# The end of a two-layer decoder trunk: the last add and square in halves, other sums and the norm weight ahead, stores on two queues

## The chip, the cores and the metric

The kernel runs on one core of a Trainium2 chip. The time is device microseconds of one execution; several executions are timed and their median is taken. A change of about 0.2% (4.55 us) is what a measurement of this kernel can tell from no change.

## The reference

Input x is 256 tokens by 2048 columns in float32, with float32 weights. Layer 0 is a norm, gated linear attention, a residual add, a norm, a SwiGLU network (width 5632) and a residual add. The stream is then normed once more and projected to keys and values that layer 1 shares. Layer 1 is a norm, stick-breaking attention, a residual add, and again a norm, a SwiGLU network and a residual add. A last norm gives the output. What matters here is the very end:

```
def rmsnorm(x, w):
    xf = xf * lax.rsqrt(jnp.mean(xf * xf, axis=-1, keepdims=True) + EPS)
    return xf.astype(x.dtype) * w
...
        h = h + swiglu(rmsnorm(h, ffn_norm_w[layer]), ffn_w_gate_up[layer], ffn_w_down[layer])
...
    return rmsnorm(h, final_norm_w)
```

The last norm needs the sum of squares of all 2048 columns of a token before any output column can be scaled, and the last columns come out of the last matmuls.

## The kernel before, in words

The 256 tokens are two token tiles of 128 (index t), one token per partition; the residual stream h stays on the chip as 128 x 2 x 2048, and its 2048 columns are worked on in four column blocks of 512 (index nb, or b).

Every weight comes from memory once, in loads of 512 KB (`load_w`, line 115, issued by SyncE into `raw`). Each float32 weight is split into a rounded part and a rest: ScalarE (ACT) casts `raw` to `hi` (line 119), VectorE (DVE) subtracts to get `lo` (line 120). A product is then three matmuls on TensorE: hi by hi, hi by lo, lo by hi, added up in a PSUM tile `acc`. `raw` has four buffers, `hi` and `lo` three each, so ACT and DVE run up to two loads ahead of TensorE and then wait until TensorE has freed a buffer.

In the SwiGLU network the hidden width is taken in three passes; the third ends with the down projection of its part. That down projection runs over the four column blocks (`residual_gemm`). For blocks 0 to 2 both token tiles share a load (`gemm_tok`, matmuls on line 137). For block 3 of the last pass all six loads are fetched first and the token tiles are done one after the other (`gemm_tok_in_turn`, matmuls on line 154), so that the end of the first tile has the second tile's matmuls beside it. Only the second tile's end stands alone at the end of the program.

When a block of a tile is summed, `evac` (line 235) adds it to h on DVE, 512 columns at once, and calls `last(nb, t)`. That squares the block on ACT with a running sum (`sumsq`, line 202; the sum is fetched by a second short ACT instruction, the read-out of the accumulator). Blocks 0 to 2 are then multiplied by the final norm's weight `fw` on DVE (line 586). For block 3, `inv_rms` adds up the four sums (line 208), scales them and adds epsilon (line 209) and raises the result to -0.5 on GpSimd (POOL, line 211), which gives r. Then the four blocks are scaled by r: blocks 0 and 2 on DVE (line 595), block 1 on ACT (line 593), block 3 on DVE with the weight in the same instruction (line 591). Each block is stored by its own DMA of 256 KB on SyncE's queue (line 596).

The weight `fw` is loaded on ACT's queue (line 579), one megabyte, the same row to all 128 partitions. In the code that line stands behind the attention's output projection. The order on each engine isn't that of the code: a planner with a timeline of its own arranges the instructions, and it issues that load some 80 us earlier, when the attention's memory becomes free. Each engine takes its instructions in the order that the planner gave them, so one that waits holds up all behind it on that engine.

Of the kernel before, what the change touches and what calls it, by code (L numbers as in the profile page):

```python
# [8 lines left out]
F32 = mybir.dt.float32  # L9
# [3 lines left out]
AF = mybir.ActivationFunctionType  # L13
ALU = mybir.AluOpType
PSUM = bass.MemoryType.PSUM

P = 128
D = 2048
S = 256
NT = S // P  # L20
KD = D // P
NB = 512
NCB = D // NB
EPS = 1e-6
# [18 lines left out]
def trunk_kernel(  # L43
# [19 lines left out]
    nc = tc.nc  # L63
    v, a, pe, g = nc.vector, nc.scalar, nc.tensor, nc.gpsimd
# [5 lines left out]
    stat = ctx.enter_context(tc.tile_pool(name="stat", bufs=2))  # L70
# [16 lines left out]
    neg_half = const.tile([P, NT], F32, name="neg_half")  # L87
# [35 lines left out]
    def gemm_tok(w_ap, kt, lhs, c0, evac, k_row0=0, before=None):  # L123

        acc = [ps_acc.tile([P, NB], F32, name="acc") for _ in range(NT)]
        k0 = 0
        while k0 < kt:
            nk = 1 if before is not None and k0 < 2 else 2
            hi, lo = load_w(w_ap, k_row0 + k0, nk, c0, NB)
            if before is not None:  # L130
                before(k0)
            for j in range(nk):
                k = k0 + j
                for t in range(NT):
                    xh, xl = lhs(k, t)
                    for n, (l, r) in enumerate(((xh, hi), (xh, lo), (xl, hi))):
                        pe.matmul(acc[t], l, r[:, j, :], start=(k == 0 and n == 0), stop=(k == kt - 1 and n == 2))  # L137
            k0 += nk
        for t in range(NT):
            evac(t, acc[t])  # L140

    def gemm_tok_in_turn(w_ap, kt, lhs, c0, evac, k_row0):

        wh, wl = (w.rearrange("p (n a) s c -> p n (a s c)", n=8)[:, i : i + 4] for w in xt_pair()[2:] for i in (0, 4))
        parts = []
        for i, k0 in enumerate(range(0, kt, 2)):
            parts.append(load_w(w_ap, k_row0 + k0, 2, c0, NB, (wh[:, i, :], wl[:, i, :]) if i < 4 else None))
        for t in range(NT):
            acc = ps_acc.tile([P, NB], F32, name="acc")
            for k in range(kt):  # L150
                xh, xl = lhs(k, t)
                hi, lo = (w[:, k % 2, :] for w in parts[k // 2])
                for n, (l, r) in enumerate(((xh, hi), (xh, lo), (xl, hi))):
                    pe.matmul(acc, l, r, start=(k == 0 and n == 0), stop=(k == kt - 1 and n == 2))  # L154
            evac(t, acc)
# [44 lines left out]
    def sumsq(ss, src):  # L200
        junk = stat.tile([P, NB], F32, name="junk")
        a.activation(junk, src, AF.Square, accum_out=ss)

    def inv_rms(ss, n, name):

        nt = ss.shape[1]
        s = stat.tile([P, nt], F32, name=f"{name}_s")
        v.tensor_reduce(s, ss, axis=mybir.AxisListType.X, op=ALU.add)
        v.tensor_scalar(s, s, 1.0 / n, EPS, ALU.mult, ALU.add)
        r = stat.tile([P, nt], F32, name=f"{name}_r")  # L210
        g.tensor_tensor(r, s, neg_half[:, :nt], ALU.pow)
        return r
# [17 lines left out]
    def residual_gemm(w_ap, kt, lhs, k_row0, after=None, after_tile=None):  # L230

        for nb in range(NCB):
            def evac(t, acc, nb=nb):
                hs = h[:, t, nb * NB : (nb + 1) * NB]
                v.tensor_tensor(hs, acc, hs, ALU.add)  # L235
                if after_tile is not None:
                    after_tile(nb, t)
            if after_tile is not None and nb == NCB - 1:
                gemm_tok_in_turn(w_ap, kt, lhs, nb * NB, evac, k_row0)
            else:  # L240
                gemm_tok(w_ap, kt, lhs, nb * NB, evac, k_row0)
            if after is not None:
                after(nb)
# [44 lines left out]
    with tc.tile_pool(name="gla", bufs=1) as gp:  # L288

        rg = gp.tile([P, NT, VW], F32, name="rg")  # L290
        ss = stat.tile([P, NT, NCB], F32, name="ss")
# [165 lines left out]
        for hd in range(GH):  # L457
# [10 lines left out]
            for t in range(NT):  # L468
                op = ps_x.tile([P, 512], F32, name="px")
# [14 lines left out]
    ss = stat.tile([P, NT, NCB], F32, name="ss")  # L484
# [5 lines left out]
    ss = stat.tile([P, NT, NCB], F32, name="ss")  # L490
# [81 lines left out]
    ss = stat.tile([P, NT, NCB], F32, name="ss")  # L572
# [3 lines left out]
    ss = stat.tile([P, NT, NCB], F32, name="ss")  # L576
    late = ctx.enter_context(tc.tile_pool(name="late", bufs=1))
    fw = late.tile([P, D], F32, name="fw")
    a.dma_start(fw, final_norm_w.rearrange("(o d) -> o d", o=1).broadcast_to([P, D]))

    def last(nb, t):
        hs = lambda b: h[:, t, b * NB : (b + 1) * NB]
        fs = lambda b: fw[:, b * NB : (b + 1) * NB]
        sumsq(ss[:, t, nb : nb + 1], hs(nb))
        if nb + 1 < NCB:
            v.tensor_tensor(hs(nb), hs(nb), fs(nb), ALU.mult)
            return
        r = inv_rms(ss[:, t : t + 1, :], D, "y")
        for b in range(NCB):
            if b == NCB - 1:  # L590
                v.scalar_tensor_tensor(hs(b), hs(b), r, fs(b), ALU.mult, ALU.mult)
            elif b % 2:
                a.mul(hs(b), hs(b), r)
            else:
                v.tensor_scalar(hs(b), hs(b), r, None, ALU.mult)
            nc.sync.dma_start(out[t * P : (t + 1) * P, b * NB : (b + 1) * NB], hs(b))

    ffn(1, fh, fl, r3, after_tile=last)


# [31 lines left out]
```

## Time and profile before

| | us |
|---|---|
| median of 3 runs | 2276.88 (2275.75 to 2277.51) |
| the profiled execution, its own time | 2274.84 |
| span of the profile | 2273.0 |
| TensorE busy with matmuls | 2256.5 (99%) |
| VectorE, ScalarE, GpSimd busy | 1246.9, 1047.3, 60.7 |

The profile gives, for one execution, each engine's busy time, the chain of work that ended last (from the last instruction back through what released it), groups of instructions by line, the waits between engines, a timeline, and a table of busy time in chosen stretches. Times are counted from the start of the span. The profiled execution's own time is somewhat longer than the span, since starting and ending lie around it.

### The profile page before, as it was taken

Reading aid. Unit: us, or ns where it says so; the run is one execution under the profiler, and the core shown is the slowest. Engines: PE = TensorE matmul, PEld = TensorE weight load, DVE = VectorE, ACT = ScalarE, POOL = GpSimd, SP = SyncE. Lnnn points to the kernel's source line nnn. Section 1 sums busy time; section 2 is a strip of 40 time slices with the busy share of each in tenths; the row PEclk is TensorE's granted clock in tenths of the full one; section 3 lists DMA queues with packets and bytes.
Section 4 is the critical chain, followed back from the end, with each engine's and each line's share of the span. In section 5 each row is a group of like instructions: output and inputs, shape, how many; then the busy total and the mean of one; then the engine's idle time right before and its main releaser. Section 6 shows DMA issues by size and latency. Waiting matters only on the chain.

```text
span 2273.0 us, 27138 instructions
## 1 busy us (share of the span) xinstructions
PE 2256.5 (99%) x10642; PEld 1887.5 (83%) x10642; DVE 1246.9 (55%) x1263; ACT 1047.3 (46%) x1225; POOL 60.7 (3%) x72
## 2 busy tenths in 40 slices
PE   9999999999999999999999999999999999999998
PEld 7888888888888888888888888888888888888887
DVE  6776555555445445444664567655445444554555
ACT  6544545444434444344554446554444344434444
POOL 2100000000000000000000111000000000000000
PEclk9999999999999999999999999999999999999999
DMA  7554555666666665666566654556666666666664
GB/s 224 171 162 148 166 167 183 188 188 190 189 194 191 189 193 188 193 192 190 183 187 193 187 183 140 166 186 188 191 191 190 194 189 191 187 193 194 192 187 158
DMA packets 242712, 419.23 MB, mean 184 GB/s; under 512 B 12972, under 2 KB 64264, under 8 KB 242456
## 3 DMA queue, kind: packets, MB, share of 16 engines
q1 hardware_dynamic: 242408, 416.44, 60.4%
q8 instruction: 83, 1.36, 0.2%
q10 hardware_dynamic: 176, 1.06, 0.1%
q14 instruction: 45, 0.37, 0.0%
HBM read 415.35 MB, written 2.10 MB: 184 GB/s over the span
## 4 chain that ended last, share of the span: by engine, by line
PE 99%; DVE 0%; issue 0%; DMA 0%; ACT 0%; SPq 0%; POOLq 0%; POOL 0%; DVEq 0%; ACTq 0%
PE acc L137 82%; PE acc L169 7%; PE acc L170 4%; PE tr L264 1%; PE px L425 1%; PE tr L194 1%; PE acc L172 0%; PE acc L154 0%; PE px L474 0%; PE px L529 0%; PE tr L560 0%; DMA h<-in_x_dram 0%; DVE B L356 0%; PE px L437 0%; PE tr L561 0%
## 5 line engine op out<-in xcount | busy, mean ns | idle before, releaser
L120 DVE TENSOR_TENSOR lo<-raw,hi 128x1024 fp32r<-128x1024 f32 (+1 forms) x783 | 971.8, 1242 | 923.9 <-ACT hi L119 923.5
L119 ACT CAST hi<-raw 128x1024 fp32r<-128x1024 f32 (+1 forms) x783 | 823.2, 1052 | 1033.9 <-PE acc L137 891.6
L137 PE MATMUL acc<-hi,xhl 128*128 128x512 f32 x4096 | 1273.0, 390 | 0.9 <-DVE xhl L185 0.7
L137 PEld LDWEIGHTS acc<-hi,xhl 128*128 128x128 f32 x4096 | 768.2, 188 | 159.6 <-ACT hi L119 1.4
L137 PE MATMUL acc<-lo,xhl 128*128 128x512 f32 x2048 | 799.5, 391 | 0.0
L137 PEld LDWEIGHTS acc<-lo,xhl 128*128 128x128 f32 x2048 | 384.8, 188 | 78.9
L137 PE MATMUL acc<-lo,hid_h 128*128 128x512 f32 x680 | 264.9, 389 | 0.0
L137 PE MATMUL acc<-hi,hid_l 128*128 128x512 f32 x680 | 264.6, 389 | 0.0
L169 PE MATMUL acc<-xhl,hi 128*128 128x512 f32 x735 | 256.2, 396 | 0.6 <-ACT hi L119 0.6
L137 PE MATMUL acc<-hi,hid_h 128*128 128x512 f32 x680 | 240.7, 390 | 0.0
L170 PE MATMUL acc<-xhl,lo 128*128 128x256 f32 x784 | 209.6, 281 | 2.2 <-DVE lo L120 2.1
L169 PEld LDWEIGHTS acc<-xhl,hi 128*128 128x128 f32 x735 | 134.8, 188 | 27.7 <-ACT hi L119 1.0
L170 PEld LDWEIGHTS acc<-xhl,lo 128*128 128x128 f32 x784 | 147.7, 189 | 8.9 <-DVE lo L120 3.1
L137 PEld LDWEIGHTS acc<-hi,hid_l 128*128 128x128 f32 x680 | 127.6, 188 | 26.4
L137 PEld LDWEIGHTS acc<-hi,hid_h 128*128 128x128 f32 x680 | 127.6, 188 | 26.3
L137 PEld LDWEIGHTS acc<-lo,hid_h 128*128 128x128 f32 x680 | 127.7, 188 | 26.1
L184 ACT ACTIVATE xhl<-tr,gains 128x256 fp32r<-128x256 f32 x96 | 40.7, 469 | 31.2 <-PE tr L194 27.6
L185 DVE SCALAR_TENSOR_TENSOR xhl<-tr,gains,xhl 128x256 fp32r<-128x256 f32 x96 | 42.4, 478 | 18.6 <-ACT xhl L184 18.6
L235 DVE TENSOR_TENSOR h<-acc,h 128x512 f32<-128x512 f32 x64 | 41.2, 682 | 7.7 <-PE acc L154 5.1
L258 ACT ACTIVATE sg<-acc,n_r 128x512 f32<-128x512 f32 x44 | 30.0, 690 | 20.8 <-PE acc L137 20.8
L267 ACT CAST hid_h<-tr 128x512 fp32r<-128x512 f32 x44 | 23.6, 589 | 31.4 <-PE tr L264 31.4
L268 DVE TENSOR_TENSOR hid_l<-tr,hid_h 128x512 fp32r<-128x512 f32 x44 | 28.3, 686 | 17.3 <-ACT hid_h L267 17.3
(170 smaller groups left out, 716.8 us busy)
## 6 DMA issues: line engine op xcount, KB each, us to landing
raw<-in_ffn_w_gate_up_dram SPq DMA_DIRECT2D x352, 512.0 KB, 3.9
raw<-in_ffn_w_down_dram SPq DMA_DIRECT2D x176, 512.0 KB, 3.7
raw<-in_gla_w_in_dram SPq DMA_DIRECT2D x97, 512.0 KB, 3.8
raw<-in_sb_w_kv_dram SPq DMA_DIRECT2D x64, 512.0 KB, 3.9
raw<-in_gla_w_out_dram SPq DMA_DIRECT2D x32, 512.0 KB, 3.7
raw<-in_sb_w_q_dram SPq DMA_DIRECT2D x32, 512.0 KB, 3.6
raw<-in_sb_w_out_dram SPq DMA_DIRECT2D x32, 512.0 KB, 3.7
h<-in_x_dram SPq DMA_DIRECT2D x8, 256.0 KB, 6.9
```

Of the source, the lines that this page charges most:

```text
L119: a.copy(hi[:, :n], raw[:, :n])
L120: v.tensor_tensor(lo[:, :n], raw[:, :n], hi.bitcast(F32)[:, :n], ALU.subtract)
L137: pe.matmul(acc[t], l, r[:, j, :], start=(k == 0 and n == 0), stop=(k == kt - 1 and n == 2))
L169: pe.matmul(acc[c], hi[:, j, cs], both, start=first, stop=False)
L170: pe.matmul(acc[c][:, :S], lo[:, j, cs], xhl[:, k0 + j, 0, :], start=False, stop=False)
L184: a.mul(dst_h, src, scale)
L185: v.scalar_tensor_tensor(dst_l, src, scale, dst_h.bitcast(F32), ALU.mult, ALU.subtract)
L194: pe.transpose(tp[:, o : o + P], src(t)[:, j * P : (j + 1) * P], ident)
L235: v.tensor_tensor(hs, acc, hs, ALU.add)
L258: a.activation(sg[t], acc, AF.Silu, scale=r[:, t : t + 1])
L267: a.copy(hh[:, :, ts], tv)
L268: v.tensor_tensor(hl[:, :, ts], tv, hh.bitcast(F32)[:, :, ts], ALU.subtract)
```

## The change

The add of a block to h moves from `evac` into `last`, which now gets the PSUM tile too. `fw` is multiplied once by the square root of 2048 (ACT), so that r can be (sum of squares + 2048 eps) to the power -0.5. Behind block 2 the sums of blocks 0 to 2 are added up and 2048 eps is added (`s3`). Block 3 is added and squared in two halves of 256 columns; its product with `fw` goes to a tile `y` on DVE; the two half sums and `s3` are added in one DVE instruction in front of the power. The scaling by r is on ACT for block 0 and on DVE for blocks 1 to 3, all four plain. Block 0 is stored on ACT's queue, the others on SyncE's.

```diff
             def evac(t, acc, nb=nb):
+                if after_tile is not None:
+                    after_tile(nb, t, acc)
+                    return
                 hs = h[:, t, nb * NB : (nb + 1) * NB]
                 v.tensor_tensor(hs, acc, hs, ALU.add)
-                if after_tile is not None:
-                    after_tile(nb, t)
...
+    a.mul(fw, fw, float(D) ** 0.5)
+    s3 = stat.tile([P, NT], F32, name="s3")
+    HB = NB // 2
+
+    def last(nb, t, acc):
         hs = lambda b: h[:, t, b * NB : (b + 1) * NB]
         fs = lambda b: fw[:, b * NB : (b + 1) * NB]
-        sumsq(ss[:, t, nb : nb + 1], hs(nb))
         if nb + 1 < NCB:
+            v.tensor_tensor(hs(nb), acc, hs(nb), ALU.add)
+            sumsq(ss[:, t, nb : nb + 1], hs(nb))
             v.tensor_tensor(hs(nb), hs(nb), fs(nb), ALU.mult)
+            if nb == NCB - 2:
+                v.tensor_reduce(s3[:, t : t + 1], ss[:, t, : NCB - 1], axis=mybir.AxisListType.X, op=ALU.add)
+                v.tensor_scalar(s3[:, t : t + 1], s3[:, t : t + 1], D * EPS, None, ALU.add)
             return
-        r = inv_rms(ss[:, t : t + 1, :], D, "y")
+        two = stat.tile([P, 2], F32, name="two")
+        for c in (0, 1):
+            part = hs(nb)[:, c * HB : (c + 1) * HB]
+            v.tensor_tensor(part, acc[:, c * HB : (c + 1) * HB], part, ALU.add)
+            junk = stat.tile([P, NB], F32, name="junk")
+            a.activation(junk[:, :HB], part, AF.Square, accum_out=two[:, c : c + 1])
+        y = late.tile([P, NB], F32, name="y", bufs=2)
+        v.tensor_tensor(y, hs(nb), fs(nb), ALU.mult)
+        r = stat.tile([P, 1], F32, name="y_r")
+        v.tensor_scalar(r, two[:, 0:1], two[:, 1:2], s3[:, t : t + 1], ALU.add, ALU.add)
+        g.tensor_tensor(r, r, neg_half[:, :1], ALU.pow)
+        rows_out = out[t * P : (t + 1) * P, :]
         for b in range(NCB):
-            if b == NCB - 1:
-                v.scalar_tensor_tensor(hs(b), hs(b), r, fs(b), ALU.mult, ALU.mult)
-            elif b % 2:
-                a.mul(hs(b), hs(b), r)
+            z = y if b == NCB - 1 else hs(b)
+            if b == 0:
+                a.mul(z, z, r)
             else:
-                v.tensor_scalar(hs(b), hs(b), r, None, ALU.mult)
-            nc.sync.dma_start(out[t * P : (t + 1) * P, b * NB : (b + 1) * NB], hs(b))
+                v.tensor_scalar(z, z, r, None, ALU.mult)
+            (a if b == 0 else nc.sync).dma_start(rows_out[:, b * NB : (b + 1) * NB], z)
```

## Rows read from the trace of the kernel before

**Rows 1.** The page's part 4: the chain that ended last, by line.
```profile
PE acc L137 82%; PE acc L169 7%; PE acc L170 4%; PE tr L264 1%; PE px L425 1%; PE tr L194 1%; PE acc L172 0%; PE acc L154 0%; PE px L474 0%; PE px L529 0%; PE tr L560 0%; DMA h<-in_x_dram 0%; DVE B L356 0%; PE px L437 0%; PE tr L561 0%
```
**Rows 2.** Waits from 1460 to 2264: engine, line, releaser: total us, times, longest.
```profile
ACT hi L119 <- PE acc L137: 399.3, 243, 2.6
```
**Rows 3.** Timeline behind the last matmul: start, us, engine, operation, count, idle before.
```profile
2264.67 0.69 DVE L235 TENSOR_TENSOR h<-acc,h 128x512 f32<-128x512 f32 x1 [3.39 <-PE acc L154]
2265.45 0.63 ACT L202 ACTIVATE junk<-h 128x512 f32<-128x512 f32 x1 [4.99 <-DVE h L235]
2265.99 0.19 ACT L202 ACTIVATION_READ_ACCUMULATOR junk<-h 128x1 f32 x1
2266.21 0.16 DVE L208 TENSOR_REDUCE y_s<-ss 128x1 f32<-128x4 f32 x1 [0.85 <-ACT junk L202]
2266.40 0.15 DVE L209 TENSOR_SCALAR y_s<-y_s 128x1 f32<-128x1 f32 x1
2266.63 0.55 POOL L211 TENSOR_TENSOR y_r<-y_s,neg_half 128x1 f32<-128x1 f32 x1 [6.93 <-DVE y_s L209]
2267.22 0.72 ACT L593 ACTIVATE h<-h,y_r 128x512 f32<-128x512 f32 x1 [1.04 <-POOL y_r L211]
2267.22 0.88 DVE L595 TENSOR_SCALAR h<-h,y_r 128x512 f32<-128x512 f32 x2 [0.67 <-POOL y_r L211]
2268.02 0.75 DVE L591 SCALAR_TENSOR_TENSOR h<-h,y_r,fw 128x512 f32<-128x512 f32 x1
```
**Rows 4.** Timeline of SyncE's queue: the second tile's first and last two store issues.
```profile
2267.73 0.33 SPq L596 DMA_DIRECT2D out_dram<-h  x1
...
2268.63 0.90 SPq L596 DMA_DIRECT2D out_dram<-h  x2
```
**Rows 5.** Table by stretch: length, engines' busy us, clock, DMA share, GB/s.
```profile
2268.40:2268.60 0.20, 0.00 (x0) 0.00 (x0) 0.20 (x1) 0.00 (x0) 0.00 (x0) 1.00 0.19 72
2268.60:2271.20 2.60, 0.00 (x0) 0.00 (x0) 0.16 (x1) 0.00 (x0) 0.00 (x0) 0.72 1.01 380
2271.50:2273.00 1.50, 0.00 (x0) 0.00 (x0) 0.00 (x0) 0.00 (x0) 0.00 (x0) 0.50 0.00 0
```
**Rows 6.** Groups of instructions by shape: count, busy us, mean ns, idle before.
```profile
L175 DVE TENSOR_TENSOR kk<-acc,kk 128x256 f32<-128x256 f32 x16 | 6.3, 424 | 5.5 <-ACT kk L174 5.5
...
L174 ACT COPY kk<-acc 128x256 f32<-128x256 f32 x16 | 5.8, 372 | 12.3 <-PE acc L172 12.3
...
L184 ACT ACTIVATE xhl<-tr,gains 128x256 fp32r<-128x256 f32 x96 | 40.7, 469 | 31.2 <-PE tr L194 27.6 <-DVE xhl L185 3.6
...
L595 DVE TENSOR_SCALAR h<-h,y_r 128x512 f32<-128x512 f32 x4 | 1.8, 483 | 1.3 <-POOL y_r L211 1.3
```
**Rows 7.** Timeline behind the third block: two adds, two Squares in a row.
```profile
2252.67 1.28 DVE L235 TENSOR_TENSOR h<-acc,h 128x512 f32<-128x512 f32 x2
2253.39 0.63 ACT L202 ACTIVATE junk<-h 128x512 f32<-128x512 f32 x1 [1.89 <-DVE h L235]
...
2254.02 0.61 ACT L202 ACTIVATE junk<-h 128x512 f32<-128x512 f32 x1
```
**Rows 8.** A 2048-column activation; the final weight's load, issue and KB with us to landing.
```profile
L353 ACT ACTIVATE lev<-lev 128x2048 f32<-128x2048 f32 x1 | 1.9, 1914 | 0.0
...
1468.20 0.36 ACTq L579 DMA_DIRECT2D fw<-in_final_norm_w_dram  x1
...
fw<-in_final_norm_w_dram ACTq DMA_DIRECT2D x1, 1024.0 KB, 6.6
```
**Rows 9.** A weight cast beside that load (timeline); the subtractions (groups by line).
```profile
1470.46 1.05 ACT L119 CAST hi<-raw 128x1024 fp32r<-128x1024 f32 x1 [1.73 <-PE acc L137]
...
L120 DVE TENSOR_TENSOR lo<-raw,hi 128x1024 fp32r<-128x1024 f32 (+1 forms) x783 | 971.8, 1242 | 923.9 <-ACT hi L119 923.5
```
**Rows 10.** Table by stretch, with two queues loading at once.
```profile
1472.00:1473.00 1.00, 1.00 (x7) 0.81 (x6) 0.78 (x1) 0.00 (x0) 0.00 (x0) 1.00 0.95 379
```
**Rows 11.** Timeline: the last block's add of the first token tile.
```profile
2257.19 0.69 DVE L235 TENSOR_TENSOR h<-acc,h 128x512 f32<-128x512 f32 x1 [1.74 <-PE acc L154]
```

More of the change, by code (lines that the diff above doesn't have):

```diff
@@ L579, in trunk_kernel @@
     a.dma_start(fw, final_norm_w.rearrange("(o d) -> o d", o=1).broadcast_to([P, D]))
-    def last(nb, t):
+    a.mul(fw, fw, float(D) ** 0.5)
+    s3 = stat.tile([P, NT], F32, name="s3")
+    HB = NB // 2
+    def last(nb, t, acc):
         hs = lambda b: h[:, t, b * NB : (b + 1) * NB]
         fs = lambda b: fw[:, b * NB : (b + 1) * NB]
-        sumsq(ss[:, t, nb : nb + 1], hs(nb))
         if nb + 1 < NCB:
+            v.tensor_tensor(hs(nb), acc, hs(nb), ALU.add)
+            sumsq(ss[:, t, nb : nb + 1], hs(nb))
             v.tensor_tensor(hs(nb), hs(nb), fs(nb), ALU.mult)
+            if nb == NCB - 2:
+                v.tensor_reduce(s3[:, t : t + 1], ss[:, t, : NCB - 1], axis=mybir.AxisListType.X, op=ALU.add)
+                v.tensor_scalar(s3[:, t : t + 1], s3[:, t : t + 1], D * EPS, None, ALU.add)
             return
-        r = inv_rms(ss[:, t : t + 1, :], D, "y")
+        two = stat.tile([P, 2], F32, name="two")
[10 more added lines that the diff above has]
+        rows_out = out[t * P : (t + 1) * P, :]
         for b in range(NCB):
-            if b == NCB - 1:
-                v.scalar_tensor_tensor(hs(b), hs(b), r, fs(b), ALU.mult, ALU.mult)
-            elif b % 2:
-                a.mul(hs(b), hs(b), r)
-            else:
-                v.tensor_scalar(hs(b), hs(b), r, None, ALU.mult)
-            nc.sync.dma_start(out[t * P : (t + 1) * P, b * NB : (b + 1) * NB], hs(b))
+            z = y if b == NCB - 1 else hs(b)
+            if b == 0:
+                a.mul(z, z, r)
+            else:
+                v.tensor_scalar(z, z, r, None, ALU.mult)
+            (a if b == 0 else nc.sync).dma_start(rows_out[:, b * NB : (b + 1) * NB], z)
     ffn(1, fh, fl, r3, after_tile=last)
```

## The prediction, made before the changed kernel ran

> **What bounds the kernel now.** The page comes first: the chain that ended last is matmuls of TensorE (PE), 82% of it on one line and most of the rest on its like [rows 1]. The waits over the last 800 us show ScalarE (ACT) waiting for TensorE to free a weight buffer, 243 times, and no TensorE wait among the long ones [rows 2]. So up to the last matmul the time is a count of matmuls, and the change touches none. An edit can only gain behind the last matmul, and only lose before it, where it makes weights late.
>
> The timeline behind the last matmul is the second view [rows 3]. With 0 at 2264.67, when the add of the last 512 columns of the second token tile begins: add to 0.69, Square from 0.78, its accumulator read out until 1.51, reduce at 1.54, multiply-add at 1.73, pow on GpSimd from 1.96 to 2.52, then at 2.55 the scaling by r: two blocks on VectorE (DVE), each 0.48, in 0.88 together, one on ACT in 0.72 beside them, the last on DVE until 4.10.
>
> Third the issues on SyncE's queue [rows 4]: the first store at 3.06, right behind the first scaled block, the others about 0.45 apart, the last about 4.4. Fourth the table by stretch [rows 5]: DMA traffic sets in within 2268.40 to 2268.60, in its last fifth; from 2268.60 to 2271.20 the 16 DMA engines at a busy share of 1.01 and 380 GB/s; from 2271.50 to the end of the span nothing. Four stores of 256 KB are 1.05 MB; at 380 GB/s that is 2.76 us. So the end is: r, first scaled block, 0.83 us from first issue to first byte (2267.73 to about 2268.56), 2.76 us of data, about 1.6 us of closing. Two things follow. What comes before the first store's issue is on the path; what comes after it isn't, as long as the DMA engines are fed. And the closing, the data and the first byte are 5.2 of the 8.33 us behind the last matmul, so even a free computation would gain only 3.1 us, 0.14%.
>
> **The change part by part.** The sum is made on the profiled execution (span 2273.0, own time 2274.84); its differences are carried to the median 2276.88, which lies 2.04 higher.
>
> *Halves.* A DVE operation of 256 columns with one source in PSUM takes 0.42, against 0.69 for 512 [rows 3, 6]. Two adds on one engine overlap by 0.1 (on the same engine two of 0.69 take 1.28 [rows 7]), so the first half is done at 0.42, the second at 0.75. The Square of 256 columns has no row. Below: 0.37, a 256-column copy on ACT from PSUM; above: 0.47, a 256-column activation with a gain per partition [rows 6]. I take 0.41: 0.63 for 512 and about 0.42 per further 512 columns in the row of 2048 (1.92 [rows 8]) make 0.42 for 256, and the copy is the nearest in work. Two Squares in a row start 0.63 apart, the read-out of the first hidden in it [rows 7]; so I let the halves start one duration apart. First Square at 0.51, second at 0.92 (its data are there at 0.84), done at 1.33; the read-out ends 0.10 later, as it does for 512 columns: 1.43, against 1.51. Halving gains only 0.08 of the 0.8 that the Square and its read-out take, because each half pays its fixed part. Bounds: 1.83 if nothing overlaps at the upper duration (Square 0.51 to 0.98, read-out 0.19, then the same again), 1.35 with 0.37 each.
>
> [...]
>
> *Sums ahead.* The reduce (0.16) and multiply-add (0.15), with their gaps 0.45 from the read-out's end to pow's start [rows 3], become one two-scalar add. No row has two scalar columns; the one-column operations of rows 3 take 0.15 to 0.16, and I take 0.15 (up to 0.2). With the same gaps, 0.03 ahead and 0.08 behind: 0.26, a gain of 0.19. The extra reduce and add for the other three blocks are moved ahead, four operations of 0.15 in all; they queue on DVE behind the third block's work, and there DVE stands idle 1.74 us before the first tile's last add [rows 11]: hidden. Without that cover they would cost 0.6 on the first tile, whose tail has the second tile's matmuls above it anyway.
>
> *y = h times weight.* 0.69 on DVE. It stands behind the second add, 0.66 to 1.35, and the waiting instruction behind it is the r sum, which wants ACT at 1.43: hidden by the Square with 0.1 to spare. If DVE takes it after the r sum instead, it lies beside pow (0.55) and delays the first scaling by some 0.1.
>
> *pow* 0.55, unchanged, now 1.69 to 2.24 against 1.96 to 2.52: 0.27 earlier.
>
> *Scaling and stores.* DVE now scales blocks 1, 2 and 3, each a plain scaling like the two of rows 3 (0.48 each [rows 6], 0.40 apart), and ACT block 0 (0.72). The fused multiply of 0.75 is gone, so the last block is ready 1.28 after r's use begins instead of 1.55. The first store still waits for a 0.48 DVE block. Blocks 1 to 3 on SyncE's queue, block 0 on ACT's, some 0.25 behind the first: the engines are fed no later than before, and 2.76 us of data follow the first byte in either case. Two queues together ran at 379 GB/s in a stretch where the weight's load on ACT's queue lay beside SyncE's [rows 10], against 380 here. So I take 0; as bounds I let the data take 7% less or more, 0.2 each way, the one more queue to be waited for at the end within that; no row asks for either.
>
> *The weight times 45.25, ahead.* One ACT operation of 128x2048 from SBUF: a row of that shape takes 1.92 [rows 8]; four times the 512-column scaling, 2.9, is the upper end. It needs the load of 1 MB that ACT issues at 1468.2 and that lands 6.6 later [rows 8]. Behind it on ACT stand the weight casts. Their cover: three buffers, a load every 2.69 us (cast 1.05 plus 1.64, the mean wait in rows 2), so a cast that starts when its buffer comes free has two loads, 5.38, until TensorE wants it; less cast 1.05 and the subtraction 1.24 [rows 9] that is 3.1 to spare. 1.92, and 2.9 as well, fit: nothing is lost if the multiply runs once the weight has landed.
>
> **Sum.** 0.08 + 0.19 = 0.27 us off the chain up to pow, nothing behind it, nothing before: own time 2274.57, median **2276.6**. With the bounds, halves done at 1.35 or 1.83 and stores 0.2 either way: from 0.55 less to 0.33 more, 2276.3 to 2277.2.
>
> **Rivals.**
> *Halves cost what they save.* Read-out at 1.83, pow at 2.09 instead of 1.96: 0.13 later, 2277.0. For it: the fixed part of 0.15 that the DVE rows show (0.42 for half of 0.69); against it: rows 7, where a read-out is overlapped.
> *Stores bound by issue, not by data.* If the last store's issue set the end, it would move from about 4.4 to 3.6 (pow done at 2.24, scaling from 2.28, last block 1.28 later): 0.8 less, 2276.1. Against: the 1.01 share in rows 5 with four stores queued.
> *Slower: the multiply holds up ACT.* Place: ACT's queue right behind the issue at 1468.2. The multiply then waits for the landing at 1474.8 and ends at 1476.7; the cast of 1470.46 [rows 9] starts there, its subtraction ends at 1479.0, and TensorE wanted it at 1470.46 + 5.38 = 1475.84. TensorE stands 3.2 us, once; the next load has room again. 2276.88 + 3.2 - 0.27 = 2279.8. It decides from a wait of 1.2 us (3.1 less 1.92); a shorter one costs nothing. For it: ACT takes instructions in order, and the kernel's planner, which lifted the load 80 us ahead of its place in the code, can lift the multiply too. Against: ACT has long idle stretches behind 1475, and a planner that knows of the transfer puts the multiply there.
> *Order upset.* The planner arranges 800 us of work after that multiply anew; a worse order of casts in the last two stages could cost TensorE 5 us or more (two loads late): 2282. Nothing in rows 2 shows it near.
>
> **How the numbers follow.** Forecast 0.64, halves for nothing 0.14, issue-bound 0.06, ACT held up (in part or whole) 0.12, order upset 0.04. A change of 0.2% is 4.55 us, and less cannot be told from none. No case but the last gets there; faster by it is excluded by the 3.1 us above and left with 0.02 for the spread between executions (2275.75 to 2277.51). Same 0.93, slower 0.05. The range takes that spread around 2276.1 to 2277.0 and most of the way to the held-up case: 2275.2 to 2279.2.
>
> **What would show it.** Right: a second Square starting 0.4 behind the first, pow starting 1.6 to 1.8 behind the last add's start, the DMA share still at 1.0 for 2.7 us, the end 0.3 earlier; the multiply on ACT between two casts, with TensorE unbroken beside it. Wrong: a TensorE gap near 1475 or in the last stage, a Square whose second half starts 0.6 behind the first, a stretch of stores shorter than 2.6 us, or any difference above 4 us, which no part here accounts for but the order upset.

## The result, and the profile after

The changed kernel takes 2290.29 us, the kernel before 2275.87 in the same session: a ratio of 1.0064, 95% interval 1.0053 to 1.0075. It is 14.4 us slower; the prediction had 0.3 faster, in a range that ended at 2279.2.

The tail came out nearly as worked out. The timeline behind the last matmul of the changed kernel (start, us, engine, line, operation, tiles, count, idle before):

```profile
2280.31 0.76 DVE L601 TENSOR_TENSOR h<-acc,h 128x256 f32<-128x256 f32 x2 [4.03 <-PE acc L154]
...
2280.76 0.42 ACT L603 ACTIVATE junk<-h 128x256 f32<-128x256 f32 x1 [5.04 <-DVE h L601]
2281.09 0.19 ACT L603 ACTIVATION_READ_ACCUMULATOR junk<-h 128x1 f32 x1
2281.09 0.69 DVE L605 TENSOR_TENSOR y<-h,fw 128x512 f32<-128x512 f32 x1
2281.18 0.40 ACT L603 ACTIVATE junk<-h 128x256 f32<-128x256 f32 x1
2281.49 0.19 ACT L603 ACTIVATION_READ_ACCUMULATOR junk<-h 128x1 f32 x1
2281.71 0.27 DVE L607 TENSOR_SCALAR y_r<-two,s 128x1 f32<-128x1 f32 x1
2282.06 0.55 POOL L608 TENSOR_TENSOR y_r<-y_r,neg_half 128x1 f32<-128x1 f32 x1 [7.09 <-DVE y_r L607]
2282.65 0.72 ACT L613 ACTIVATE h<-h,y_r 128x512 f32<-128x512 f32 x1 [0.97 <-POOL y_r L608]
2282.65 0.88 DVE L615 TENSOR_SCALAR h<-h,y_r 128x512 f32<-128x512 f32 x2 [0.67 <-POOL y_r L608]
```

Pow starts 1.75 us behind the first add (before 1.96 [rows 3], predicted 1.69), and the span ends 8.09 behind it (2280.31 to 2288.4) instead of 8.33. So the end of the program gained 0.2 us, and what is lost is lost ahead of it: the first add of the end starts at 2280.31, before at 2264.67.

There TensorE still reads as busy throughout. The tables by stretch of the two kernels, before and then after, show what the busy share hides (length, PE, PEld, DVE, ACT, POOL busy with counts, clock, DMA share, GB/s; 606 to 690 is the first down projection, 1600 to 1700 lies in the last layer's gate and up projections):

```profile
606.00:690.00 84.00, 84.00 (x372) 69.55 (x371) 42.76 (x39) 32.39 (x32) 0.00 (x0) 1.00 0.63 194
1600.00:1700.00 100.00, 100.00 (x451) 82.97 (x450) 49.31 (x44) 43.96 (x47) 0.00 (x0) 1.00 0.63 190
```

```profile
606.00:690.00 84.00, 84.00 (x362) 67.74 (x361) 41.55 (x38) 31.46 (x30) 0.00 (x0) 1.00 0.60 187
1600.00:1700.00 100.00, 100.00 (x451) 82.96 (x450) 49.52 (x45) 42.98 (x45) 0.00 (x0) 1.00 0.63 190
```

In the down projection the same 84 us hold 362 matmuls instead of 372, at a granted clock of 1.00 in both; in the gate and up projections nothing changes. The down projection of 606 us belongs to the first layer, whose work the change doesn't touch and which runs some 870 us ahead of the first instruction that differs. The groups by line name the operands, before and then after (count, busy us, mean ns). Behind `acc<-` stand the streamed tile, 512 columns of weights from `hi` or `lo`, and the stationary tile, a 128x128 block that a weight load (PEld) of its own brings in for each matmul (for the first line below 4096 loads of 188 ns on average beside 4096 matmuls): `xhl` holds the normed activations in two parts, `hid_h` and `hid_l` the two parts of the SwiGLU network's hidden values, which the down projection multiplies (the hidden tiles).

```profile
L137 PE MATMUL acc<-hi,xhl 128*128 128x512 f32 x4096 | 1273.0, 390 | 0.9 <-DVE xhl L185 0.7 <-ACT xhl L184 0.2
...
L137 PE MATMUL acc<-lo,hid_h 128*128 128x512 f32 x680 | 264.9, 389 | 0.0
L137 PE MATMUL acc<-hi,hid_l 128*128 128x512 f32 x680 | 264.6, 389 | 0.0
```

```profile
L137 PE MATMUL acc<-hi,xhl 128*128 128x512 f32 x4096 | 1273.5, 391 | 0.5 <-DVE xhl L185 0.3 <-ACT xhl L184 0.2
...
L137 PE MATMUL acc<-hi,hid_l 128*128 128x512 f32 x680 | 269.5, 396 | 0.0
L137 PE MATMUL acc<-lo,hid_h 128*128 128x512 f32 x680 | 268.5, 395 | 0.0
```

The matmuls whose stationary operand is a hidden tile take 6 to 7 ns more on average; those of xhl don't. The timeline of TensorE gives the spacing of starts, before and then after:

```profile
640.82 0.39 PE L137 MATMUL acc<-hi,hid_l 128*128 128x512 f32 x1
641.04 0.39 PE L137 MATMUL acc<-lo,hid_h 128*128 128x512 f32 x1
...
642.40 0.39 PE L137 MATMUL acc<-lo,hid_h 128*128 128x512 f32 x1
```

```profile
640.74 0.39 PE L137 MATMUL acc<-lo,hid_h 128*128 128x512 f32 x1
640.97 0.40 PE L137 MATMUL acc<-hi,hid_l 128*128 128x512 f32 x1
...
642.37 0.40 PE L137 MATMUL acc<-hi,hid_l 128*128 128x512 f32 x1
```

Seven spacings are 1.58 us before and 1.63 after: 226 and 233 ns. There are 2112 such matmuls (44 slices of the hidden width, 4 column blocks, 2 token tiles, 3 products, 2 layers), and 6 to 7 ns for each is 12.7 to 14.8 us, against a loss of 14.4: all of it, or nearly all.

What the two programs differ in there is the place of the tiles. The new statistics tiles (`s3` and `two` in, `y_s` out) make their pool 64 bytes larger, and all behind it moves up. Byte addresses in each partition, as the two programs allot them (no trace shows them):

```
              before    after
xhl            35360    35360
hi (first)    117280   117280
lo (first)    129568   129568
hid_h (first) 149536   149600
```

### The profile page after: what moved, and what is told of

Same layout as the page of the kernel before. It is cut to its first block, busy times and chain, and to the rows that moved or that the text cites. A ratio compares the mean times of both kernels' runs of the same rounds, so it can differ in the third digit from the quotient of the medians.

```text
span 2288.4 us, 27149 instructions
## 1 busy us (share of the span) xinstructions
PE 2272.5 (99%) x10642; PEld 1889.9 (83%) x10642; DVE 1248.5 (55%) x1269; ACT 1048.4 (46%) x1230; POOL 60.8 (3%) x72
## 3 DMA queue, kind: packets, MB, share of 16 engines
q10 hardware_dynamic: 464, 1.58, 0.2%
## 4 chain that ended last, share of the span: by engine, by line
PE 99%; DVE 0%; issue 0%; DMA 0%; ACT 0%; SPq 0%; POOLq 0%; POOL 0%; DVEq 0%; ACTq 0%
PE acc L137 82%; PE acc L169 7%; PE acc L170 4%; PE tr L265 1%; PE px L426 1%; PE tr L194 1%; PE acc L172 0%; PE acc L154 0%; PE px L475 0%; PE px L530 0%; PE tr L561 0%; DMA h<-in_x_dram 0%; DVE B L357 0%; PE px L438 0%; PE tr L562 0%
## 5 line engine op out<-in xcount | busy, mean ns | idle before, releaser
L137 PE MATMUL acc<-hi,hid_l 128*128 128x512 f32 x680 | 269.5, 396 | 0.0
L238 DVE TENSOR_TENSOR h<-acc,h 128x512 f32<-128x512 f32 x56 | 36.0, 682 | 2.6 <-PE acc L137 2.5
```

## The experiments

Before them stood theory P (the hidden tiles' place sets the speed of their matmuls) against rival O (the change's own instructions, or the planner's order of them).

**The shift alone.** One line, in the kernel before, ahead of the `late` pool:

```diff
+    stat.tile([P, 16], F32, name="pad", bufs=1)
```

> The kernel before, with one unused tile of 64 bytes at the end of the statistics pool. No instruction and no order differs; every tile that lies behind that pool (hid_h, hid_l, sg, vv, kk and others) moves up by 64 bytes, as it does in the changed kernel. Theory P (place): the changed kernel is slow because the down projections read their stationary operands hid_h and hid_l from addresses 64 bytes further up, 7 ns more for each of 2112 matmuls: this kernel takes 2290 us too, with hid matmuls at 396 ns instead of 389. Rival O (order): the changed kernel's own instructions or the planner's order of them cost the time: 2276 us, hid matmuls at 389 ns.

2290.89 us, ratio 1.0066 (1.0051 to 1.0081). With the same instructions in the same order as before, an unused tile costs all that the change cost, and the groups match the changed kernel's:

```profile
L137 PE MATMUL acc<-hi,xhl 128*128 128x512 f32 x4096 | 1273.5, 391 | 1.0 <-ACT xhl L184 1.0
...
L137 PE MATMUL acc<-hi,hid_l 128*128 128x512 f32 x680 | 269.5, 396 | 0.0
```

P holds, O falls.

**Other shifts of the same kind.** `[P, 16]` in the changed kernel (hidden tiles at 128 above their old place), `[P, 8]` and `[P, 24]` in the kernel before (32 and 96):

```diff
+    stat.tile([P, 8], F32, name="pad", bufs=1)
```

> The changed kernel with the same unused tile of 64 bytes, so that hid_h lies 128 bytes above its place in the kernel before, and again at 32 modulo 128. Theory P, with a period of 128 bytes or a divisor of it: 2275.6 us, 0.2 to 0.3 under the kernel before, hid matmuls at 389 ns. Theory P with a longer period (256 bytes or more): anything from 2276 to 2290. Rival O: 2290 us.

> The kernel before with 32 unused bytes: hid_h at 64 modulo 128 (before: 32, changed kernel: 96). Theory P says that the time depends on the address: if 64 is a good boundary, hid matmuls at 389 ns or under it, 2276 us or less; if the slowdown grows with the distance from the old place, between 2276 and 2290 us. Rival O: 2276 us.

> The kernel before with 96 unused bytes: hid_h at 0 modulo 128, as aligned as it can be. [...] Rival O: 2276 us.

2287.09 (1.0051, 1.0036 to 1.0066), 2291.39 (1.0068, 1.0051 to 1.0084) and 2292.83 us (1.0076, 1.0061 to 1.0091). All three cost time: no period of 128 bytes, and the rounder address (96 bytes up, 0 modulo 128) is no better. In the kernel before, xhl, hi, lo and hid all lie at 32 modulo 512, which leaves two readings: distances (R) or own addresses (A).

**Everything moved together.** All but h by 64 up, and all but h and two constant tiles (`ident`, `ones`) by 32 down:

```diff
     h = const.tile([P, NT, D], F32, name="h")
+    const.tile([P, 16], F32, name="front")
```

> The kernel before with 64 unused bytes right behind h: the activations xhl, the weights raw, hi and lo and the hidden tiles hid_h and hid_l all move up by the same 64 bytes (to 96 modulo 512). No instruction and no order differs. Theory R: what counts is the distance between the stationary operand and the streamed operand of a matmul, a multiple of 512 bytes in the kernel before and not in the slow ones; the distances stay, so 2276 us, hid matmuls at 389 ns. Rival A: what counts is each operand's own address (32 modulo 512 is good); then all matmuls slow down by 6 to 7 ns, some 10,000 of them, 2340 us, xhl matmuls at 397 ns; or only those of hid if only that region matters, 2290.

```diff
-    neg_half = const.tile([P, NT], F32, name="neg_half")
-    g.memset(neg_half, -0.5)
...
-    gains = const.tile([P, sum(n for _, _, n in rows)], F32, name="gains")
+    n_gains = sum(n for _, _, n in rows)
+    gains = const.tile([P, n_gains + NT], F32, name="gains")
+    neg_half = gains[:, n_gains:]
+    g.memset(neg_half, -0.5)
```

> The kernel before with neg_half in two spare columns of the tile of gains, which moves xhl, raw, hi, lo and the hidden tiles all down by 32 bytes, to 0 modulo 512. Theory R: 2276 us, no difference, the distances stay. [...]

2275.79 (1.0000, 0.9990 to 1.0009) and 2276.29 us (1.0001, 0.9992 to 1.0009). No difference: with all at 96, at 0 or at 32 modulo 512 the time is the same, so a tile's own address doesn't count, and A falls.

**The hidden tiles alone.** `[P, 64]`, `[P, 48]` and `[P, 56]` (256, 192 and 224 bytes) at the front of the SwiGLU network's pool:

```diff
         with tc.tile_pool(name=f"ffn{layer}", bufs=2) as fp:
+            fp.tile([P, 64], F32, name="pad", bufs=1)
```

> The kernel before with 256 unused bytes at the front of the pool of the SwiGLU network: only hid_h, hid_l and sg move, by 256 bytes. It measures the period. If 256 bytes (or a divisor that the runs before left open) is the period: 2276 us, hid matmuls at 389 ns. If the period is 512 bytes or more: 2285 to 2292 us, hid matmuls at 395 ns or more, under theory R and rival A alike.

> As the run with the hidden tiles moved by 256 bytes, but by 192: is any distance that is not a multiple of 256 slow (32, 64, 96 and 128 were)? Theory R: 2288 to 2292 us, hid matmuls at 395 ns or more. Rival: only distances below 128 plus a little collide, 2276 us.

> As the runs with the hidden tiles moved by 192 and 256 bytes, but by 224. Theory R, with a cost that falls toward the next multiple of 256 (32 to 96: 7 to 8 ns, 128: 5.5, 192: 2.4, 256: 0): 1 ns a matmul, 2277 to 2280 us. Rival (any distance but a multiple of 256 costs at least what 192 does): 2281 or more.

256: 2275.95 us (0.9999, 0.9990 to 1.0008), no cost. 192: 2281.29 (1.0022, 1.0013 to 1.0032), a third of the cost, which neither side had said. 224: 2289.89 (1.0060, 1.0043 to 1.0076): the idea that the cost falls steadily toward 256 was wrong. The period is 256 bytes, and within it the cost isn't a slope.

**Hi and lo moved away from xhl.**

```diff
     wsp = ctx.enter_context(tc.tile_pool(name="wsp", bufs=3))
+    wsp.tile([P, 16], F32, name="front", bufs=1)
```

> The kernel before with 64 unused bytes in front of the tiles hi and lo: hi, lo and all behind them, the hidden tiles among them, move up by 64 bytes; xhl and raw stay. Theory R (distance of the stationary operand from the streamed one): now hid keeps its distance from hi and lo and its matmuls stay at 389 ns, while xhl loses it, so the matmuls of xhl with hi and lo (6144 on line 137, and 1568 with the roles exchanged on lines 169 to 172) take 6 to 7 ns more: 2276 + 41 + 10 = 2327 us. Rival B (distance of the hidden tiles from the buffers that the DMAs write, or from xhl): the hid matmuls slow down, those of xhl don't, 2290 us.

2290.96 us (1.0065, 1.0048 to 1.0081), nearly the rival's number, but the groups say otherwise (line numbers are one higher):

```profile
L138 PE MATMUL acc<-hi,xhl 128*128 128x512 f32 x4096 | 1282.1, 393 | 0.7 <-ACT xhl L185 0.7
L138 PE MATMUL acc<-lo,xhl 128*128 128x512 f32 x2048 | 803.9, 393 | 0.0
...
L138 PE MATMUL acc<-hi,hid_l 128*128 128x512 f32 x680 | 264.6, 389 | 0.0
...
L155 PE MATMUL acc<-xhl,hid_h 128*128 128x512 f32 x32 | 10.2, 394 | 0.0
```

The hidden tiles, moved but at their old distance from hi and lo, are fast; xhl, unmoved, is slow. That is R and not B, with 2 to 3 ns each where 7 were expected. The last line is a control within the run: of the last block's six weight loads four lie in an xhl tile, which didn't move, and over these the same hidden tiles, now 64 above, take 394 ns; in the kernel before they took 389.

One part of R isn't borne out. On lines 169 to 172 the roles are exchanged: a weight tile is stationary, xhl is streamed, and the stationary tile now lies 64 above the streamed one. Line 169 before, and its like in this run:

```profile
L169 PE MATMUL acc<-xhl,hi 128*128 128x512 f32 x735 | 256.2, 396 | 0.6 <-ACT hi L119 0.6
```

```profile
L170 PE MATMUL acc<-xhl,hi 128*128 128x512 f32 x735 | 259.6, 399 | 0.6 <-ACT hi L120 0.6
```

That is 3 ns more and not 7, where runs that leave this distance alone spread from 395 to 398; the 49 of line 172 even fell from 399 to 395.

Seen from the weights xhl now lies 64 bytes below, which is 192 modulo 256, the cheap distance of the run above. So the sign should count, and the next run asked for it: xhl moved by 64 modulo 256, hi, lo and hid by a multiple of 256 (64 bytes ahead of xhl, 192 ahead of hi, and 512 saved by one shared buffer for the gains).

```diff
+    xt.tile([P, 16], F32, name="front", bufs=1)
...
+    wsp.tile([P, 48], F32, name="middle", bufs=1)
...
-        gains_in = const.tile([n_rows, P], F32, name=name)
+        gains_in = const.tile([n_rows, P], F32, name=name, tag="gains_in")
```

> The kernel before with xhl 64 bytes (modulo 256) above hi, lo and the hidden tiles, which keep their distances of multiples of 256 among themselves (the two input tiles of gains share one buffer, so that it fits). Theory R, signed: what costs is the distance of the stationary operand from the streamed one, modulo 256 and with its sign: 64 costs 7 ns a matmul (the hidden tiles showed it), 192 costs 2 to 3. Then 6144 matmuls with xhl stationary and weights streamed take 7 ns more, 43 us, and some 1568 with the roles exchanged 2 to 3 ns more, 4 us: 2318 to 2326 us; hid matmuls on line 137 stay at 389 ns. Rival S (the hidden tiles' region is special, and xhl's distance costs little whatever its sign, as the run with hi and lo moved by 64 may be read): 2288 to 2294 us.

2314.86 us (1.0172, 1.0157 to 1.0187), 38.8 more than before: R with its sign, 3 us under its range, and S falls. Spread over the 6144 matmuls with xhl stationary that is 6.3 ns each; those with the roles exchanged add little (line 169's mean is 397 here). The groups (line numbers two higher):

```profile
L139 PE MATMUL acc<-hi,xhl 128*128 128x512 f32 x4096 | 1296.6, 396 | 1.1 <-ACT xhl L186 1.1
L139 PE MATMUL acc<-lo,xhl 128*128 128x512 f32 x2048 | 811.9, 397 | 0.0
...
L139 PE MATMUL acc<-hi,hid_l 128*128 128x512 f32 x680 | 264.6, 389 | 0.0
```

**The change with its tiles in the old places.**

```diff
-    s3 = stat.tile([P, NT], F32, name="s3")
+    s3 = stat.tile([P, NT], F32, name="s3", tag="o_s")
```

> The changed kernel with s3 in the buffers of a statistics tile of the first stage, dead by then, so that the pool is no larger than before and the hidden tiles lie where they lay. The rest of the change stands. Theory P (place, under R and A alike): 2275.6 us, 0.15 to 0.3 under the kernel before, from the shorter end alone, hid matmuls at 389 ns. Rival: some of the 14 us belongs to the 4096 bytes that the second layer's hidden tiles moved, or to the order: 2280 or more.

2275.54 us over 11 runs, 2276.15 before: ratio 0.9997 (0.9988 to 1.0005). All 14 us are back. It beats the changed kernel and can't be told from the one before; the hidden tiles' matmuls are back at 389 ns:

```profile
L137 PE MATMUL acc<-hi,hid_l 128*128 128x512 f32 x680 | 264.6, 389 | 0.0
```

In the profile its end takes 8.14 us behind the first add (2265.76 to 2273.9), before 8.33. The 4096 bytes that `y` moves the second layer's hidden tiles are a multiple of 256 and cost nothing.

**Two parts of it undone**, each in that kernel: one queue, and the block in one piece.

```diff
-            (a if b == 0 else nc.sync).dma_start(rows_out[:, b * NB : (b + 1) * NB], z)
+            nc.sync.dma_start(rows_out[:, b * NB : (b + 1) * NB], z)
```

> The changed kernel with its tiles in the old places, and all stores on SyncE's queue; block 0 is still scaled on ACT. The prediction's step (the data bound the end, a second queue gives nothing): 2275.5 us as with two queues, four stores' data still in 2.7 to 2.8 us behind the first byte. Rival (the second queue helps): 0.3 to 0.5 later behind the first issue.

```diff
-        for c in (0, 1):
...
+        v.tensor_tensor(hs(nb), acc, hs(nb), ALU.add)
+        sumsq(two[:, 0:1], hs(nb))
...
-        v.tensor_scalar(r, two[:, 0:1], two[:, 1:2], s3[:, t : t + 1], ALU.add, ALU.add)
+        v.tensor_scalar(r, two[:, 0:1], s3[:, t : t + 1], None, ALU.add)
```

> The changed kernel with its tiles in the old places, and the last block added and squared in one piece as before (one sum plus s3 in front of pow). The prediction's step (halving gains 0.08): Square's read-out ends 1.51 behind the first add's start instead of 1.36 to 1.43; as the add of two sums took 0.27 with two scalar columns and takes 0.15 with one, pow starts at 1.77, about where the halves have it, and the time is the same 2275.5. Rival (halves pay in full): pow 0.1 to 0.2 earlier than with halves.

2275.83 (0.9999, 0.9990 to 1.0008) and 2275.95 us (0.9998, 0.9989 to 1.0008): times can't tell them apart, and the profiles hardly. With one queue the end takes 8.12 us (2265.18 to 2273.3), with two 8.14. In one piece pow starts 1.78 behind the first add, with halves 1.76; but with halves and one queue it starts at 1.81, so the difference is within the spread between kernels that should be alike there. The timelines in one piece, with halves in the old places, and with halves and one queue:

```profile
2266.04 0.69 DVE L599 TENSOR_TENSOR h<-acc,h 128x512 f32<-128x512 f32 x1 [3.78 <-PE acc L154]
...
2267.52 0.21 DVE L604 TENSOR_SCALAR y_r<-two,s 128x1 f32<-128x1 f32 x1
2267.82 0.55 POOL L605 TENSOR_TENSOR y_r<-y_r,neg_half 128x1 f32<-128x1 f32 x1 [6.87 <-DVE y_r L604]
```

```profile
2265.76 0.76 DVE L601 TENSOR_TENSOR h<-acc,h 128x256 f32<-128x256 f32 x2 [3.80 <-PE acc L154]
...
2267.17 0.27 DVE L607 TENSOR_SCALAR y_r<-two,s 128x1 f32<-128x1 f32 x1
2267.52 0.55 POOL L608 TENSOR_TENSOR y_r<-y_r,neg_half 128x1 f32<-128x1 f32 x1 [6.87 <-DVE y_r L607]
```

```profile
2265.18 0.76 DVE L601 TENSOR_TENSOR h<-acc,h 128x256 f32<-128x256 f32 x2 [3.80 <-PE acc L154]
...
2266.99 0.55 POOL L608 TENSOR_TENSOR y_r<-y_r,neg_half 128x1 f32<-128x1 f32 x1 [6.92 <-DVE y_r L607]
```

## Why the prediction was wrong

The step that failed is the first: "So up to the last matmul the time is a count of matmuls, and the change touches none." The count stayed; the price of 2112 of them didn't. The diff allots new tiles in a pool that lies ahead of the hidden tiles, and the prediction costed every instruction of the diff and no byte of it. Its "nothing before it" in the sum should have been plus 13 to 15 (2112 matmuls, 6 to 7 ns; the unused tile alone cost 14.9), and an edit can lose ahead of the last matmul without any weight coming late. "Order upset", to which the slow side was left, was a wrong mechanism too: the programs give TensorE the same matmuls in the same order and ACT the same casts, with the multiply put in and a different end, and none of it costs time (the change in the old places).

What the prediction said of the diff itself held in the main:

- *Halves.* 0.08 was forecast. The Squares took 0.42 and 0.40, 0.42 apart, and the read-out ended at 1.37 (predicted 1.43, before 1.51). The piece beside it was mis-sized: the sum with two scalar columns takes 0.27, not 0.15. The 0.15 was that of line 209, whose scalars are both constants; with one column it takes 0.21, so each column costs 0.06, and the second takes back most of the 0.08. Against the block in one piece halving is worth nothing that can be told: 1.75, 1.76 and 1.81 to pow with halves, 1.78 without. What kept the gain small is the price of a half: 0.42 and 0.40 against 0.63 for the whole [rows 3], 0.19 more for the two. It was no loss either, since the first half (0.45 to 0.87) runs beside the second's add, which ends at 0.76.
- *Sums ahead.* With the block in one piece they alone bring pow from 1.96 to 1.78, 0.18 of 0.19 forecast; together with the halves 0.21 in the changed kernel, of 0.27.
- *Stores.* The data bound the end, as said: 380 GB/s at a share of 1.02, as before [rows 5]. The changed kernel's table:

```profile
2284.00:2286.60 2.60, 0.00 (x0) 0.00 (x0) 0.00 (x0) 0.00 (x0) 0.00 (x0) 0.55 1.02 380
```

- *The weight's multiply.* ACT did wait in its queue for the load, and longer than the 1.2 us from which the rival was to decide: 1.8 in the changed kernel, 2.5 in that with the old places. That an engine holds back a ready instruction behind one that waits shows early in the kernel before: DVE waited 2.48 us for ACT's cast, until 6.75, and took the cast of a mask on line 329 only behind that subtraction, at 7.36, though its input was written by 5.13. The cast behind that of 1470.46 [rows 9] in the kernel before, and then the rows of the change in the old places:

```profile
1474.09 1.05 ACT L119 CAST hi<-raw 128x1024 fp32r<-128x1024 f32 x1 [2.57 <-PE acc L137]
```

```profile
1471.56 1.05 ACT L119 CAST hi<-raw 128x1024 fp32r<-128x1024 f32 x1 [1.73 <-PE acc L137]
1475.09 1.92 ACT L583 ACTIVATE fw<-fw 128x2048 f32<-128x2048 f32 x1 [2.48 <-DMA fw<-in_final_norm_w_dram]
1476.91 1.98 ACT L119 CAST hi<-raw 128x1024 fp32r<-128x1024 f32 x2
```

  It cost nothing, because the cast of 1471.56 had gone ahead of it and the wait lay where ACT in the kernel before stood idle for TensorE anyway (2.57). The next cast came 5.35 us behind that one instead of 3.63, so it lost 1.7 us, less than the 3.1 to spare: the point should have been counted from the next cast's due start, not from the multiply's.

## What to carry to other kernels

A tile added to a pool moves all that lies behind it, so a diff is read for bytes as well as for instructions: compare the addresses of the operands of the busiest matmuls, and the distance between the two of a matmul, before and after. Where a stage that the change doesn't touch runs slower with its engine as busy as ever, count instructions in a fixed stretch, and test it with an unused tile of the same size. Here the cure was to put the new sums into the buffers of a dead tile.

## What the runs showed of the hardware

The time of a 128x512 float32r matmul with a fresh 128x128 stationary operand depends on the distance, modulo 256 bytes, of the stationary tile from the streamed one; this is shown with activations stationary and weights streamed. With the hidden tiles stationary (cost in us over the kernel before, divided by 2112 matmuls; for 128 over the change in the old places):

| distance in bytes | us over | ns per matmul |
|---|---|---|
| 0, 256 | -0.2 | 0 |
| 32 | 15.4 | 7.3 |
| 64 | 14.9 | 7.1 |
| 96 | 16.9 | 8.0 |
| 128 | 11.6 | 5.5 |
| 192 | 5.0 | 2.4 |
| 224 | 13.8 | 6.6 |

The mean times of the groups agree within about 1 ns. The intervals of the ratios come to 1.6 to 1.8 ns either way (1 ns at 0, 256 and 192), so 192 stands apart from the others; whether 32, 64, 96, 128 and 224 differ among themselves is not settled by the times. The same with xhl stationary: 6 ns at 64 in the groups (390 to 396), 2 to 3 at 192. With the weights stationary and xhl streamed 64 cost at most some 3 ns (396 to 399), and why is open. The granted clock is 1.00 in the stretches shown and 0.998 to 0.999 over each whole execution, and the weight loads keep their 0.19 us. Why the distance counts no run shows; why 192 is cheaper than 128 and 224 stays open, and distances that aren't multiples of 32 weren't tried.
